# Second score matmul over 128 rows instead of 64, exponentials in place, and fewer buffers, in a hybrid decoder block

## The chip, the cores and the metric

The kernel runs on one core of one Trainium2 chip. The metric is the device time of one execution in microseconds (us); lower is better. The kernel before is a Tile program: the code below is traced once, a scheduler puts each engine's instructions into one fixed order, and at run time every engine works through its own list in that order and waits on semaphores for the others. The engines are TensorE (PE, whose weight loads the profile lists apart as PEld), VectorE (DVE), ScalarE (ACT) and GpSimd (POOL); SyncE (SP) issues all the DMAs.

## The reference, cut to what matters

One decoder block over 1024 tokens of width 1024: an RMSNorm and one large projection, then two attention branches whose outputs are gated, merged and projected, then a SwiGLU feed-forward. The change touches the two attention branches alone:

```python
# branch A, sparse: 8 heads of 64; every query row attends to its own 256 keys
sc = jnp.einsum('bqhd,bqkhd->bhqk', qb, kg) * att_scale
p = softmax(where(valid, sc, -inf));  out = p @ vg
# branch B, differential: 4 heads of two maps, 64 dims each
sc = jnp.einsum('bqhmd,bshmd->bhmqs', qb, k) * scale
a = softmax(where(causal, sc, -inf))
a = a[:, :, 0] - lam * a[:, :, 1];  out = a @ v
...
merged = gates[:, :, 0] * (o_a @ w_branch_dsa) + gates[:, :, 1] * (o_b @ w_branch_diff)
```

Everything is float32. The kernel keeps precision by splitting a number into a high part, which the TensorE format float32r holds, and a low part, the rest; a product is then hi x hi + lo x hi + hi x lo.

## The kernel before, in words

The kernel runs in stages that follow each other on TensorE: transposes and index projection; the large projections (L427, L505) with the sparse branch's key selection beside them on VectorE; from 529 us the attention; from 843 us the merge (L632) and the output projection (L882); and the feed-forward (L933, L914) to the end.

Attention consists of 32 units of the differential branch (4 heads, 8 blocks of 128 queries each, the longest rows first) and then 64 units of the sparse branch (8 heads, 8 blocks each). A loop (L803) emits for step i the parts of several units, each part with a lag in steps: the scores of a unit at lag 0, the combination of its maps or its division at lag 1, its transposes and its product with v later. In the differential branch a unit has two maps, m = 0 and m = 1.

`scores` (L586) fills a PSUM tile `big` (two of them) with the scores of one map for one block, of up to two halves of up to 512 columns. For each half there are two matmuls that accumulate in the same place:

- L593 contracts 128 rows. Its weights are the query tile `qs`, in which the 64 rows of this map's own half (rows m*64 to m*64+63) hold the high part and the other 64 the low part (`load_maps`, L530). Its moving operand `khs` holds the high part of the keys twice, in rows 0 to 63 and in 64 to 127. So it gives q_hi x k_hi + q_lo x k_hi.
- L594 contracts the 64 rows `own` alone, where `qs` holds the high part of the queries and `kls` the low part of the keys: q_hi x k_lo. One `kls` tile serves two maps, each in its own 64 rows.

Then VectorE adds the mask, takes the row's extreme and writes the masked scores to an SBUF tile `ms` (L651 in the differential branch, L703 in the sparse one; `ms` has 3 buffers). ScalarE reads `ms` and writes the exponentials (L656, L707) to another tile: `pm0`, 3 buffers, or for map 1 one of the 4 `wide` buffers. The transposed tiles and one square (L684) also live in `wide`. The differential branch combines the two maps on VectorE (L671 to L674), TensorE transposes (L603) and multiplies with v (L610), and ScalarE copies both out (L604, L682). The sparse branch scales (L713, L715), transposes (L729), splits into two parts (L730, shown as L101 on ACT and L102 on DVE) and multiplies (L742).

At the end of each differential head its outputs, one `gt` tile of 4 KB a partition (pool `gst`, 2 buffers), are squared, normed (L685 to L690), transposed (L617) and split. During the sparse branch the differential branch's projection (L770) runs in 16 half chunks; it needs the 4 tiles of w_bdiff in both parts. `Weights.get` (L121) makes these: a DMA into a raw tile, a copy to the high part on ACT (L101), a subtraction to the low part on POOL (L102). The pool `w2` has one raw buffer of its own for that. The weights w_bdsa of the other projection are loaded likewise near the end of attention, two through the raw buffer and two through `gt` tiles.

SP's queue is one list: the loads of the next head's queries and keys, of its v, and of the weights stand in one order, and a load whose buffer is still in use holds up all that stand behind it.

Of the kernel before, what the change touches and what calls it, by code (L numbers as in the profile page):

```python
# [18 lines left out]
P = 128  # L19
# [7 lines left out]
# block whose scores are kept negated and in reverse, so that the few left out are taken away instead  # L27
# [23 lines left out]
def block_kernel(ctx, tc, x, pos, g_mix, w_qk, w_v, q_scale, w_idx, w_gate, ikg, ikb, lams, sub_g, gate_b,  # L51
# [19 lines left out]
    # constants  # L71
# [32 lines left out]
    # scratch in DRAM  # L104
    # rows (dim, map): maps 0-7 are queries, 8-15 keys
# [3 lines left out]
    # sparse branch: per head the two parts of v, high part first in even heads, last in odd ones  # L109
# [21 lines left out]
    # rows of tokens -> RMSNorm * gain, then both parts of the transpose  # L131
# [9 lines left out]
    def to_T(h, hi, lo, wide=False):  # L141
        # hi, lo: [P, KC, P] views
# [34 lines left out]
    def rope(eng, pool, xv, tabs, half, **kw):  # L177
        # xv: [P, ..., d] view; tabs: c0, c1, s0, s1 broadcast to the rotated halves
# [176 lines left out]
    # rotary tables: [c | c] and [-s | s] per position  # L355
# [43 lines left out]
    # lambda (on every partition), negated  # L399
# [130 lines left out]
    def load_maps(br, h):  # L530
        kl_ = stk.tile([P, S], F32R, name="kls", bufs=2)
        for m in range(2):
            q = stk.tile([P, S], F32R, name="qs")
            kh_ = stk.tile([P, S], F32R, name="khs")
            for j in range(2):
                rows = slice(j * 64, j * 64 + 64)
                nc.sync.dma_start(q[rows].bitcast(F32), (qk_hi if j == m else qk_lo)[br][:, 2 * h + m, :])
                nc.sync.dma_start(kh_[rows].bitcast(F32), qk_hi[br][:, 8 + 2 * h + m, :])
            own = slice(m * 64, m * 64 + 64)
            nc.sync.dma_start(kl_[own].bitcast(F32), qk_lo[br][:, 8 + 2 * h + m, :])  # L540
            maps[br, 2 * h + m] = q, kh_, kl_, own
# [9 lines left out]
    def load_head(br, h):  # L551
        # diff: head h has two maps; sparse: a pair of heads
# [21 lines left out]
    at = ExitStack()  # L574
    W2 = Weights(at.enter_context(tc.tile_pool(name="w2", bufs=1)), 1, 4)
# [4 lines left out]
    # the other branch's projection runs in half chunks, one every EVERY units of the sparse branch; until it  # L580
    # is through, the sparse outputs (head pairs below PARKED) wait in DRAM
# [4 lines left out]
    def scores(mp, t):  # L586
        q, kh_, kl_, own = mp
# [3 lines left out]
        for u in range(nh):  # L591
            cols = slice(u * w, u * w + n)
            T.matmul(sp_[:, u, :n], lhsT=q[:, t * P:(t + 1) * P], rhs=kh_[:, cols], start=True, stop=False)  # L593
            T.matmul(sp_[:, u, :n], lhsT=q[own, t * P:(t + 1) * P], rhs=kl_[own, cols], start=False, stop=True)  # L594
# [52 lines left out]
    def diff_Q(u, m):  # L647
        sv, nh = scores(maps[0, 2 * u.h + m], u.t)
        ms = ap_.tile([P, S], F32, name="ms", bufs=3)
# [389 lines left out]
```

## Time and profile before

| | us |
|---|---|
| median of 3 runs | 1743.11 (1740.65 to 1744.91) |
| span of the profiled execution | 1738.8 |
| attention in it, first score matmul to the merge | 529 to 843 |
| differential branch | 529 to 653 |
| sparse branch | 653 to 843 |

The profiled execution's own time stands in no list beside the span; the median of the runs is 4.3 us above the span, and that difference is taken for what lies around it. TensorE is busy for 98% of the span. Busy is not the same as streaming, though: a matmul counts as busy from its recorded start to its modelled end, so in a stretch that reads 100% the distance from one matmul's start to the next one's start tells how long it really held the engine.

### The profile page before, as it was taken

How to read it: one execution, taken by the hardware profiler on the slowest of the kernel's cores; microseconds unless marked ns; L12 is line 12 of the kernel's file. 1: busy time of each engine (PE TensorE's matmuls, PEld its weight loads, DVE VectorE, ACT ScalarE, POOL GpSimd, SP SyncE). 2: the span in 40 equal slices, each digit the busy share in tenths (PEclk: the TensorE clock that was granted, in tenths of full speed). 3: DMA queues.
4: the chain of work that ended last, by engine and by line, in shares of the span. 5: the costliest groups of instructions: out<-in, count | busy, mean ns of one | idle time of the engine just before them, and what ended most of it. 6: DMA issues, size and time to landing. Idle time of an engine off the chain costs nothing.

```text
span 1738.8 us, 22187 instructions
## 1 busy us (share of the span) xinstructions
PE 1699.2 (98%) x8552; PEld 1397.9 (80%) x8552; DVE 1103.3 (63%) x1901; ACT 571.9 (33%) x1035; POOL 422.1 (24%) x313
## 2 busy tenths in 40 slices
PE   7799999999999999999999999999999999999998
PEld 7688789988886677777789978888888888888886
DVE  6589999989997887777661534443443444444435
ACT  5444531221115777667520421111111111111113
POOL 2532521432201132113312222212212212211211
PEclk9999999999998999999999999999999999999999
DMA  4243342475312546544471121111111111111102
GB/s 163 88 146 110 122 139 92 134 198 153 106 52 62 124 112 159 154 137 146 149 257 49 43 79 49 61 37 49 61 37 45 56 47 37 51 59 37 37 12 97
DMA packets 69641, 162.74 MB, mean 94 GB/s; under 512 B 8096, under 2 KB 25632, under 8 KB 69536
## 3 DMA queue, kind: packets, MB, share of 16 engines
q1 hardware_dynamic: 69536, 161.33, 29.8%
q8 instruction: 67, 1.10, 0.3%
q14 instruction: 38, 0.31, 0.1%
HBM read 118.31 MB, written 42.99 MB: 93 GB/s over the span
## 4 chain that ended last, share of the span: by engine, by line
PE 86%; DVE 8%; issue 2%; DMA 1%; POOL 1%; ACT 1%; SPq 0%; DVEq 0%; POOLq 0%; ACTq 0%
PE big L933 28%; PE big L427 10%; PE tr L914 7%; PE mm L914 7%; PE mm L505 5%; PE mm L882 5%; PE mm L427 5%; PE big L594 4%; PE big L593 3%; PE mm L770 3%; PE mm L742 2%; PE mm L610 2%; PE tr L729 2%; DVE score L300 1%; DVE score L277 1%
## 5 line engine op out<-in xcount | busy, mean ns | idle before, releaser
L102 POOL TENSOR_TENSOR wlo<-raw,whi 128x1024 fp32r<-128x1024 f32 (+1 forms) x121 | 293.0, 2425 | 948.3 <-ACT whi L101 937.8
L101 ACT ACTIVATE whi<-raw 128x1024 fp32r<-128x1024 f32 (+1 forms) x124 | 129.7, 1048 | 523.8 <-issue 231.1
L918 DVE TENSOR_TENSOR x<-tr,x 128x512 f32<-128x512 f32 x168 | 115.7, 689 | 178.5 <-PE tr L914 178.0
L933 PE MATMUL big<-actC,whi 128*128 128x512 f32 x704 | 221.8, 395 | 0.0
L933 PE MATMUL big<-actA,whi 128*128 128x512 f32 x704 | 217.8, 390 | 0.0
L943 DVE TENSOR_TENSOR si<-big,si 128x512 f32<-128x512 f32 x44 | 30.4, 692 | 232.7 <-PE big L933 232.7
L299 DVE MAX8 m<-score 128x8 f32<-128x640 f32 (+5 forms) x176 | 162.6, 924 | 5.4 <-POOL score L283 0.4
L300 DVE MATCH_REPLACE8 score<-m,score 128x640 f32<-128x640 f32 (+5 forms) x176 | 159.5, 906 | 0.0
L933 PEld LDWEIGHTS big<-actC,whi 128*128 128x128 f32 x704 | 132.0, 188 | 32.0 <-ACT si L938 0.3
L933 PEld LDWEIGHTS big<-actA,whi 128*128 128x128 f32 x704 | 132.0, 188 | 28.9 <-ACT si L938 0.5
L933 PE MATMUL big<-actC,wlo 128*128 128x512 f32 x352 | 139.1, 395 | 0.0
L933 PE MATMUL big<-actA,wlo 128*128 128x512 f32 x352 | 137.1, 390 | 0.0
L918 DVE TENSOR_TENSOR x<-mm,x 128x512 f32<-128x512 f32 x168 | 115.6, 688 | 0.7
L914 PE MATMUL tr<-whi,actB 128*128 128x512 f32 x352 | 110.6, 394 | 0.0
L914 PE MATMUL mm<-whi,actB 128*128 128x512 f32 x352 | 110.4, 395 | 0.0
L427 PE MATMUL mm<-hT_hi,whi 128*128 128x512 f32 x256 | 102.4, 400 | 2.4 <-DVE st_lo L489 2.4
L427 PE MATMUL mm<-hT_lo,whi 128*128 128x512 f32 x256 | 100.8, 394 | 0.0
L427 PE MATMUL mm<-hT_hi,wlo 128*128 128x512 f32 x256 | 100.7, 393 | 0.0
L427 PE MATMUL big<-hT_hi,whi 128*128 128x512 f32 x256 | 99.6, 389 | 0.0
L427 PE MATMUL big<-hT_lo,whi 128*128 128x512 f32 x256 | 99.6, 389 | 0.0
L427 PE MATMUL big<-hT_hi,wlo 128*128 128x512 f32 x256 | 99.6, 389 | 0.0
L101 ACT ACTIVATE actB<-si 128x512 fp32r<-128x512 f32 x44 | 27.9, 634 | 196.8 <-DVE si L943 196.8
(237 smaller groups left out, 3541.6 us busy)
## 6 DMA issues: line engine op xcount, KB each, us to landing
raw<-in_w_ffi_dram SPq DMA_DIRECT2D x44, 512.0 KB, 3.4
raw<-in_w_ffo_dram SPq DMA_DIRECT2D x22, 512.0 KB, 3.4
raw<-in_w_qk_dram SPq DMA_DIRECT2D x16, 512.0 KB, 3.3
qkh<-st_hi SPq DMA_DIRECT2D x32, 256.0 KB, 2.0
qkl<-st_lo SPq DMA_DIRECT2D x32, 256.0 KB, 2.2
raw<-in_w_gate_dram SPq DMA_DIRECT2D x16, 512.0 KB, 4.3
khs<-qkh SPq DMA_DIRECT2D x32, 256.0 KB, 5.5
gdr<-gt SPq DMA_DIRECT2D x16, 512.0 KB, 3.6
```

The lines of the kernel that those rows point to most:

```text
L101: A.activation(hi, src, AF.Copy)
L102: lo_eng.tensor_sub(lo, src, hi.bitcast(F32))
L299: tc.keep_in_program_order(V.max(m8, work[t]))
L300: V.match_replace(work[t], m8, work[t], GONE)
L427: T.matmul(dst, lhsT=w[b][:, k * P:(k + 1) * P], rhs=hT[a][:, k, u * 512:(u + 1) * 512], start=n == 0, stop=n == 23)
L505: T.matmul(pt[:, tt, :], lhsT=hT[a][:, k, t * P:(t + 1) * P], rhs=wt[w0 + k // 4][b][:, (k % 4) * 256:(k % 4) * 256 + 256], start=n == 0, ...
L593: T.matmul(sp_[:, u, :n], lhsT=q[:, t * P:(t + 1) * P], rhs=kh_[:, cols], start=True, stop=False)
L594: T.matmul(sp_[:, u, :n], lhsT=q[own, t * P:(t + 1) * P], rhs=kl_[own, cols], start=False, stop=True)
L882: T.matmul(pt[:, :256], lhsT=act[a][:, k, i % 4 * P:i % 4 * P + P], rhs=wot[2 * q + k // 4][b][:, (k % 4) * 256:(k % 4) * 256 + 256], star ...
L914: T.matmul(pt, lhsT=a_[a][:, i * P:(i + 1) * P], rhs=w[b][:, u * 512:(u + 1) * 512], start=n == 0, stop=n == 3 * len(items) - 1)
L918: V.tensor_add(x2[i][:, sl], pt, x2[i][:, sl])
L933: T.matmul(gu[:, j, :], lhsT=w[b][:, k * P:(k + 1) * P], rhs=h2[u][a][:, k, :], start=n == 0, stop=n == 23)
```

## The change

- `load_maps` loads the low part of the keys twice, into both halves of a `kls` tile of its own for each map (4 buffers of 4 KB instead of 2), and the second score matmul contracts all 128 rows of `qs` and `kls`. It adds q_lo x k_lo to the scores, which the kernel before left out. Columns and number of the matmuls stay.
- The tiles `ms` and `pm0` (3 buffers each) become one tile `pm` with 5: VectorE writes the masked scores to it and ScalarE writes the exponentials over them. For map 1 of the differential branch both go to the `wide` buffer, which is so taken at the mask and no longer at the exponential.
- The raw buffer of the pool `w2` is gone. All eight weight tiles of the two branch projections are loaded into `gt` tiles, of which there are two.

Per partition that is 8 KB more, and 4 KB and 4 KB less. In the changed file the lines from L531 on carry numbers lower by one to three (L593 for L594, L650 for L651, L767 for L770).

```diff
     def load_maps(br, h):
-        kl_ = stk.tile([P, S], F32R, name="kls", bufs=2)
         for m in range(2):
             q = stk.tile([P, S], F32R, name="qs")
             kh_ = stk.tile([P, S], F32R, name="khs")
+            kl_ = stk.tile([P, S], F32R, name="kls")
             for j in range(2):
                 rows = slice(j * 64, j * 64 + 64)
                 nc.sync.dma_start(q[rows].bitcast(F32), (qk_hi if j == m else qk_lo)[br][:, 2 * h + m, :])
                 nc.sync.dma_start(kh_[rows].bitcast(F32), qk_hi[br][:, 8 + 2 * h + m, :])
-            own = slice(m * 64, m * 64 + 64)
-            nc.sync.dma_start(kl_[own].bitcast(F32), qk_lo[br][:, 8 + 2 * h + m, :])
-            maps[br, 2 * h + m] = q, kh_, kl_, own
+                nc.sync.dma_start(kl_[rows].bitcast(F32), qk_lo[br][:, 8 + 2 * h + m, :])
+            maps[br, 2 * h + m] = q, kh_, kl_
...
-    W2 = Weights(at.enter_context(tc.tile_pool(name="w2", bufs=1)), 1, 4)
+    W2 = Weights(at.enter_context(tc.tile_pool(name="w2", bufs=1)), 0, 4)
...
             T.matmul(sp_[:, u, :n], lhsT=q[:, t * P:(t + 1) * P], rhs=kh_[:, cols], start=True, stop=False)
-            T.matmul(sp_[:, u, :n], lhsT=q[own, t * P:(t + 1) * P], rhs=kl_[own, cols], start=False, stop=True)
+            T.matmul(sp_[:, u, :n], lhsT=q[:, t * P:(t + 1) * P], rhs=kl_[:, cols], start=False, stop=True)
...
     def diff_Q(u, m):
         sv, nh = scores(maps[0, 2 * u.h + m], u.t)
-        ms = ap_.tile([P, S], F32, name="ms", bufs=3)
+        pm = ap_.tile([P, 2, S], F32, name="wide", bufs=4)[:, 0, :] if m else ap_.tile([P, S], F32, name="pm", bufs=5)
...
-        pm = ap_.tile([P, 2, S], F32, name="wide", bufs=4)[:, 0, :] if m else ap_.tile([P, S], F32, name="pm0", bufs=3)
         sm = small.tile([P, 1], F32, name="sm")
-        A.activation(pm[:, :u.ext], ms[:, :u.ext], AF.Exp, bias=mx, scale=-1.0, accum_out=sm)
+        A.activation(pm[:, :u.ext], pm[:, :u.ext], AF.Exp, bias=mx, scale=-1.0, accum_out=sm)
...
-                u.wb.extend(W2.get(w_bdiff[k]) for k in range(4))
+                u.wb.extend(W2.get(w_bdiff[k], raw=gst.tile([P, S], F32, name="gt")) for k in range(4))
...
     def dsa_A(u):
-        ms = ap_.tile([P, S], F32, name="ms", bufs=3)
-        msv = ms[:, :u.ext].rearrange("p (u w) -> p u w", u=nh)
+        u.pm = ap_.tile([P, S], F32, name="pm", bufs=5)
+        msv = u.pm[:, :u.ext].rearrange("p (u w) -> p u w", u=nh)
...
-        u.pm = ap_.tile([P, S], F32, name="pm0", bufs=3)
-        A.activation(u.pm[:, :u.ext], ms[:, :u.ext], AF.Exp, bias=mx, scale=-1.0, accum_out=u.sm)
+        A.activation(u.pm[:, :u.ext], u.pm[:, :u.ext], AF.Exp, bias=mx, scale=-1.0, accum_out=u.sm)
...
-            wa.extend(W2.get(w_bdsa[k], raw=None if k % 2 else gst.tile([P, S], F32, name="gt")) for k in range(4))
+            wa.extend(W2.get(w_bdsa[k], raw=gst.tile([P, S], F32, name="gt")) for k in range(4))
```

The order of most engines stays nearly as it was. Two places change. The first is SP's queue: the last of the four loads of w_bdiff stood before the loads of the sparse heads (`qkh_77` there is the sparse branch's keys), and the other three earlier. Before:

```order
L538 DMA khs<-qkh_76 64x1024
L540 DMA kls<-qkl_78 64x1024
L547 DMA vt<-vsdr 128x8x128
L125 DMA raw<-in_w_bdiff_dram 128x1024
L538 DMA khs<-qkh_77 64x1024
L537 DMA qs<-qkh_77 64x1024
L537 DMA qs<-qkl_79 64x1024
```

Now, in the queue of the changed kernel, all four stand among the loads of the second sparse pair, the first of them behind that pair's first load:

```order
L546 DMA vt<-vsdr 128x8x128
L538 DMA khs<-qkh_77 64x1024
L125 DMA gt<-in_w_bdiff_dram 128x1024
L537 DMA qs<-qkh_77 64x1024
L539 DMA kls<-qkl_79 64x1024
L537 DMA qs<-qkl_79 64x1024
L125 DMA gt<-in_w_bdiff_dram 128x1024
L538 DMA khs<-qkh_77 64x1024
L539 DMA kls<-qkl_79 64x1024
L537 DMA qs<-qkl_79 64x1024
L125 DMA gt<-in_w_bdiff_dram 128x1024
```

So the four loads moved from the course of the differential branch to its end. The second place is POOL's list at the same point. Before, the last two low parts of w_bdiff (`wlo<-raw`) stood between the norms of the first three heads (L685, L690):

```order
L690 TENSOR_TENSOR gt<-gt,rs_5166 128x1024
L102 TENSOR_TENSOR wlo<-raw,whi 128x1024
L685 TENSOR_TENSOR wide<-gt 128x1024
L98 TENSOR_TENSOR rs_5535<-rs_v,nhalf 128x8
L690 TENSOR_TENSOR gt<-gt,rs_5535 128x1024
L102 TENSOR_TENSOR wlo<-raw,whi 128x1024
L685 TENSOR_TENSOR wide<-gt 128x1024
L98 TENSOR_TENSOR rs_5904<-rs_v,nhalf 128x8
L690 TENSOR_TENSOR gt<-gt,rs_5904 128x1024
```

Now all four follow the norm of the third head (the first row here); the first two stand ahead of the fourth head's norm (L683, L688), the last two behind it:

```order
L688 TENSOR_TENSOR gt<-gt,rs_5863 128x1024
L102 TENSOR_TENSOR wlo<-gt,whi 128x1024
L720 MEMSET wide 128x128 x2
L102 TENSOR_TENSOR wlo<-gt,whi 128x1024
L683 TENSOR_TENSOR wide<-gt 128x1024
L720 MEMSET wide 128x128 x2
L98 TENSOR_TENSOR rs_6210<-rs_v,nhalf 128x8
L688 TENSOR_TENSOR gt<-gt,rs_6210 128x1024
L720 MEMSET wide 128x128 x2
L102 TENSOR_TENSOR wlo<-gt,whi 128x1024
L102 TENSOR_TENSOR so_6278<-aux,so_6277 64x256
```

The low parts moved behind the norms; on TensorE the first half chunk of the projection that reads them keeps its place, around the transposes of the fourth head.

## Rows read from the trace of the kernel before

**Rows 1.** Page, busy time, share of the span and instructions of each engine.

```profile
PE 1699.2 (98%) x8552; PEld 1397.9 (80%) x8552; DVE 1103.3 (63%) x1901; ACT 571.9 (33%) x1035; POOL 422.1 (24%) x313
```

**Rows 2.** Busy us of each engine in eight stretches of attention, then TensorE's granted clock.

```profile
529.00:561.00 32.00, 32.00 (x126) 20.63 (x126) 21.99 (x62) 21.88 (x47) 3.52 (x2) 0.79 0.17 54
561.00:577.00 16.00, 16.00 (x72) 9.74 (x71) 10.85 (x27) 10.77 (x25) 1.74 (x1) 1.00 0.74 157
577.00:592.00 15.00, 15.00 (x99) 12.03 (x99) 14.49 (x40) 11.28 (x31) 5.54 (x4) 1.00 0.36 104
592.00:607.00 15.00, 15.00 (x67) 9.11 (x65) 10.50 (x27) 10.92 (x26) 2.27 (x1) 1.00 0.70 143
607.00:622.00 15.00, 15.00 (x96) 11.81 (x96) 14.48 (x40) 11.34 (x30) 5.43 (x3) 1.00 0.32 96
622.00:637.00 15.00, 15.00 (x70) 9.24 (x68) 10.47 (x30) 10.89 (x26) 2.36 (x1) 1.00 0.71 150
637.00:653.00 16.00, 16.00 (x104) 12.56 (x103) 15.47 (x42) 11.43 (x31) 5.42 (x3) 1.00 0.33 97
653.00:843.00 190.00, 188.48 (x1005) 139.65 (x1004) 145.61 (x365) 135.61 (x323) 48.97 (x97) 0.99 0.51 142
```

**Rows 3.** Timeline of PE: start us, length us, what, idle time before it.

```profile
559.66 0.36 PE L593 MATMUL big<-khs,qs 128*128 128x256 f32 x1
559.96 0.38 PE L594 MATMUL big<-kls,qs 64*128 64x256 f32 x1
560.27 1.38 PE L610 MATMUL mm<-vt,wide 128*128 128x128 f32 x10
561.41 0.48 PE L593 MATMUL big<-khs,qs 128*128 128x512 f32 x1
561.82 0.49 PE L594 MATMUL big<-kls,qs 64*128 64x512 f32 x1
562.24 0.49 PE L593 MATMUL big<-khs,qs 128*128 128x512 f32 x1
```

**Rows 4.** Timeline of PEld, the weight loads of the last two matmuls above.

```profile
561.82 0.18 PEld L594 LDWEIGHTS big<-kls,qs 64*128 64x128 f32 x1 [0.24 <-issue]
562.24 0.19 PEld L593 LDWEIGHTS big<-khs,qs 128*128 128x128 f32 x1 [0.24 <-issue]
```

**Rows 5.** Timeline of PE where 128-row matmuls follow one another in the sparse branch.

```profile
692.25 2.14 PE L742 MATMUL mm<-wide,vt 128*128 128x256 f32 x16
694.23 0.40 PE L770 MATMUL mm<-oT_hi,whi 128*128 128x512 f32 x1
694.46 0.40 PE L770 MATMUL mm<-oT_lo,whi 128*128 128x512 f32 x1
```

**Rows 6.** Groups by line, PEld, 653:843: count, busy us, mean ns, idle before.

```profile
L770 PEld LDWEIGHTS mm<-oT_lo,whi 128*128 128x128 f32 x64 | 12.1, 188 | 1.7
```

**Rows 7.** Line L594's matmuls: count and ns min/median/max, first and last start.

```profile
L594 PE MATMUL big<-kls,qs x192: 378/442/686, 529.0 to 836.7; 64*128 64x512 f32 x48, 64*128 64x384 f32 x48, 64*128 64x448 f32 x32, 64*128 64x320 f32 x32
```

**Rows 8.** Groups by line, DVE, 529:653; last is the idle time before and its releaser.

```profile
L651 DVE CUSTOM_DVE_ANT_0 ms<-big,causw 128x1024 f32<-128x1024 f32 (+7 forms) x64 | 47.8, 748 | 21.8 <-PE big L594 21.7
```

**Rows 9.** Timeline of PE: the third head's transposes and the projection's first matmul.

```profile
649.97 1.09 PE L617 MATMUL tr<-ident,gt 128*128 128x128 f32 x8
...
674.67 0.40 PE L770 MATMUL mm<-oT_hi,whi 128*128 128x512 f32 x1
```

**Rows 10.** Timeline of SP's queue: the first load of the second sparse pair.

```profile
649.76 0.45 SPq L538 DMA_DIRECT2D khs<-qkh  x1
```

**Rows 11.** The four loads of w_bdiff: issue ns min/median/max, first and last, landing.

```profile
L125 SPq DMA_DIRECT2D raw<-in_w_bdiff_dram x4: 333/429/527, 528.9 to 607.2; - x4
...
DMA to landing us min/median/max: 3.4/4.2/4.9
```

**Rows 12.** Timeline of ACT: the high part of one w_bdiff tile.

```profile
542.20 1.04 ACT L101 ACTIVATE whi<-raw 128x1024 fp32r<-128x1024 f32 x1
```

**Rows 13.** Timeline of POOL: the low part of one w_bdiff tile.

```profile
560.32 2.42 POOL L102 TENSOR_TENSOR wlo<-raw,whi 128x1024 fp32r<-128x1024 f32 x1 [14.15 <-ACT whi L101]
```

More of the change, by code (lines that the diff above doesn't have):

```diff
@@ L586, in scores @@
     def scores(mp, t):
-        q, kh_, kl_, own = mp
+        q, kh_, kl_ = mp
         nh, w = halves(t)
@@ L648, in diff_Q @@
         sv, nh = scores(maps[0, 2 * u.h + m], u.t)
-        ms = ap_.tile([P, S], F32, name="ms", bufs=3)
+        pm = ap_.tile([P, 2, S], F32, name="wide", bufs=4)[:, 0, :] if m else ap_.tile([P, S], F32, name="pm", bufs=5)
         mx = small.tile([P, 1], F32, name="mx")
-        V.tensor_tensor_reduce(ms[:, :u.ext].rearrange("p (u w) -> p u w", u=nh), sv,
+        V.tensor_tensor_reduce(pm[:, :u.ext].rearrange("p (u w) -> p u w", u=nh), sv,
                                causw[:, S - u.ext:].rearrange("p (u w) -> p u w", u=nh), 1.0,
                                -FILL, OP.add, OP.min, accum_out=mx)
-        pm = ap_.tile([P, 2, S], F32, name="wide", bufs=4)[:, 0, :] if m else ap_.tile([P, S], F32, name="pm0", bufs=3)
         sm = small.tile([P, 1], F32, name="sm")
-        A.activation(pm[:, :u.ext], ms[:, :u.ext], AF.Exp, bias=mx, scale=-1.0, accum_out=sm)
+        A.activation(pm[:, :u.ext], pm[:, :u.ext], AF.Exp, bias=mx, scale=-1.0, accum_out=sm)
         u.pm.append(pm)
```

## The prediction, made before the changed kernel was run

> **What bounds the kernel now.** I read the page's busy times first: TensorE is busy for 98% of the span, VectorE for 63% [rows 1]. So time can only be won on TensorE, or lost by a wait that TensorE does not have now. The change touches attention alone, so next come the busy times by stretch [rows 2]. TensorE reads 100% in nearly all of it, VectorE between 66% and 97%, ScalarE about 70%. A busy TensorE need not stream, so I then read the starts in its timeline. Where score matmuls alternate, from a 128-row L593 to a 64-row L594 and back, 512 columns are 0.41 to 0.42 us from start to start; for 256 columns it is 0.30 and 0.31 [rows 3]. Where 128-row matmuls follow one another, 512 columns take 0.23 us, and sixteen of 256 columns take 1.98 us, 0.124 each [rows 5]. So a score matmul holds the engine some 0.185 us longer than its columns need, whatever its width. The weight loads say why: each of the score loads starts at the same time as its matmul, after the load unit sat idle for 0.24 us, and takes 0.18 to 0.19 us [rows 4]. The loads of L770 take as long (188 ns) and have next to no idle time before them [rows 6]: they run under the matmul before. So the load is exposed where the number of rows switches between 128 and 64, and hidden where it stays.
>
> **The change part by part.**
>
> *Second matmul over 128 rows.* There are 192 of L594 [rows 7], as many L593, and half of each lies in either branch (8 maps or heads with 12 halves each). Columns stay, the switch goes: 384 x 0.185 = 71 us less of TensorE's time, 35.5 in each branch. The first matmul after a score gains a little too; I leave that for the range. What is late next decides how much of the 71 us reaches the end, so I take the branches apart.
>
> Differential branch, 529 to 653, 124 us. TensorE would need 124 - 35.5 = 88.5, VectorE's sum over the seven stretches is 98.3 and ScalarE's 88.5 [rows 2]. In three of them (577 to 592, 607 to 622, 637 to 653; 46 us, the short query blocks) VectorE already is at 97%: nothing to win there. In the other four, 78 us, VectorE is busy for 53.8 and ScalarE for 54.5. At the 97% that VectorE now reaches in its full stretches that would be 56 us; since two engines that feed each other would both have to be full, I take 92%, 59 us. Gain 19, between 10 (both at 80%) and 26 (VectorE without a gap). VectorE's present wait for L594, 21.7 us over 64 reductions [rows 8], is the cover that this uses up.
>
> In the first stretch TensorE's granted clock averages 0.79 [rows 2], so it ran at the lower of its two levels (1.2 GHz) for some 13 of the 32 us (32 x 0.21 / 0.5). If the clock stays up there now, that is part of these 19 us and not more, since VectorE paces the stretch.
>
> Sparse branch, 653 to 843, 190 us. TensorE needs 190 - 35.5 - 1.5 (its present idle) = 153, VectorE 145.6, ScalarE 135.6 [rows 2]. TensorE stays the bound, with VectorE close behind. At 95% of TensorE that is 161: gain 29, between 15 and 37 (no gap at all).
>
> *Keys loaded twice.* 16 more loads of 256 KB on SP, 0.45 us or a little more of its queue each [rows 10], 7 us in all, spread over the loads of 8 heads and pairs. Nothing: the loop asks for them a whole head ahead, and that head (some 30 us, 124 / 4) is the cover; a head whose loads came late would cost the lateness, at most 1 us each.
>
> *Exponentials over the scores.* Same number, shape and engine of instructions. Map 1 now takes its `wide` buffer at the reduction, so VectorE instead of ScalarE waits for that buffer, that is for a product with v four units back, with the next reductions, and through them TensorE's `big`, queued behind. No row shows that wait. The nearest is VectorE's wait for scores, 0.34 us per reduction [rows 8]; 32 of these would be 11 us, the other end is a gain of the same kind, since map 0 has five buffers instead of three. I take 0, as TensorE will be ahead of VectorE in this branch.
>
> *w_bdiff through the `gt` tiles.* This is the part that costs. Today the four loads go out between 529 and 607 us [rows 11], and all is ready 50 us before the first L770 at 674.67 [rows 9]. Now the first load stands in SP's queue behind the first load of the second sparse pair, which went out at 649.76 [rows 10], and needs the `gt` tile that the third head's transposes free at 649.97 + 1.09 [rows 9]. The other `gt` tile holds the fourth head's output until its own transposes, which stand between the projection's eighth and ninth matmul. So all four go through one tile, one after another: issue 0.5, landing 4.2 [rows 11], high part 1.04 [rows 12], low part 2.42 [rows 13], and about 0.8 of hand-overs by my estimate: 9 us each. The third high part is there 18 + 5.7 = 24 us after the start, the fourth low part after 36. The projection's first matmul comes 24 us after the start today; with less in between on TensorE and VectorE I expect 18. Its seventh matmul needs the third high part, its twelfth the fourth low part some 5 us later: TensorE would wait 6 at the first and 5 to 7 more by the last, 13 at most. ScalarE has the four copies in its list with exponentials behind them; the wait is the same chain, not a second one. Part of it falls where TensorE would have waited for VectorE anyway, so I take 8 of 0 to 13. w_bdsa goes the same way at the end, through two tiles that are both free, when nine of the 64 units are left (9 x 190 / 64 = 27 us) to cover two steps of 9 us: nothing.
>
> *Sum.* -19 - 29 + 8 = -40 us on the profiled execution's span of 1738.8, 1699; with the 4 us by which the runs' median lies over that span, 1703.
>
> **A rule against it.** Rows 4 and 6 show a weight load that waits for the matmul before it and one that does not. The Trainium skill (TensorE: Matmul & The Clock Gate, "What overlaps and what doesn't") says that a load overlaps a running matmul only when its row group differs. By that rule a 128-row load would be exposed behind a 128-row matmul too, and the new pairs would take 0.42 us as the old ones do; L770's loads [rows 5, 6] speak against it.
>
> **The rivals.**
>
> *The distance stays (slower).* If the pairs stay at 0.42 us, because the exposed load hangs on something else in them than the number of rows (weights that are read twice, accumulation into one bank), nothing is won on TensorE, and the chain of w_bdiff costs its 8 to 13 us: 1743 + 10 = 1753. It decides for slower as soon as less than 8 us of the 71 come through. For it: no row shows two 128-row score matmuls in a row. Against: L770 accumulates into one bank as well and L742 changes weights for each matmul, both at full pace [rows 5]. In the sentence above the page's rule gives this same time.
>
> *TensorE's gain comes through whole.* VectorE and ScalarE run without gaps, the chain hides behind VectorE's backlog: -26 - 37 = -63, 1680. For it: VectorE does reach 97% in three stretches. Against: in these, TensorE had no slack of its own to lose.
>
> *New waits eat most of it.* Attention becomes a ring of three nearly full engines with two `big` tiles: gains of 10 and 15, the chain at its full 13: -12, 1731. For it: VectorE's and ScalarE's sums are so close to TensorE's new one. Against: TensorE runs at 99% today with VectorE at 77%.
>
> **How the numbers follow.** Forecast 1703 (within about 15): 0.62. Whole gain, 1680: 0.14. New waits, 1731: 0.15. Distance stays, 1753: 0.09. The range leaves out the last case and the far ends of the next two: 1684 to 1731. About 0.3%, 5 us, is what a measurement can tell from no change. Under 1738 lie the first two cases and most of the third: faster 0.87; same 0.05; slower 0.08.
>
> **What would show it.** In the new trace, 512-column scores start 0.23 us after one another where TensorE does not wait, and the loads of the second matmul have no 0.24 us of idle before them; if not, the first step is wrong. In the differential branch VectorE is at 90% and more and TensorE waits for `big` on VectorE, in about 105 us; the sparse branch takes about 169 us with the chain. TensorE waits at the projection's seventh to twelfth matmul for the high and low parts of w_bdiff; if these waits are missing, the chain was priced too high. The prediction is wrong if ScalarE's blocked list or the `wide` buffers stop VectorE by more than 10 us in either branch, or if the clock falls to its lower level in stretches where TensorE now waits.

## The result, and the profile after

The changed kernel takes 1701.5 us, the median of four runs (1700.1 to 1703.2); the kernel before, in the same comparison, 1741.9 (1739.5 to 1744.9). The ratio is 0.9762, with a 95% interval from 0.9738 to 0.9786: 40 us faster. The forecast was 1703, in a range from 1684 to 1731. The profiled execution spans 1701.5 us, against 1738.8.

The page's busy times and its chain of waits answer to [rows 1]. TensorE's busy share falls from 98% to 96%. In the chain TensorE has 76% of the span and VectorE 13%; the page of before has 86% and 8%.

```profile
PE 1639.8 (96%) x8552; PEld 1392.5 (82%) x8552; DVE 1097.4 (64%) x1901; ACT 568.7 (33%) x1035; POOL 421.8 (25%) x313
...
PE 76%; DVE 13%; DMA 3%; issue 3%; ACT 2%; POOL 2%; SPq 0%; DVEq 0%; POOLq 0%; ACTq 0%
```

The first question is the distance of the score matmuls. The timeline of PE at the start of attention shows the changed kernel's first scores (L592 and L593 are the old L593 and L594) behind the last projection matmuls (L427):

```profile
528.50 0.39 PE L427 MATMUL big<-hT_lo,whi 128*128 128x512 f32 x1
528.73 0.40 PE L427 MATMUL big<-hT_hi,wlo 128*128 128x512 f32 x1
528.96 0.39 PE L592 MATMUL big<-khs,qs 128*128 128x512 f32 x1
529.19 0.39 PE L593 MATMUL big<-kls,qs 128*128 128x512 f32 x1
529.42 0.39 PE L592 MATMUL big<-khs,qs 128*128 128x512 f32 x1
529.64 0.39 PE L593 MATMUL big<-kls,qs 128*128 128x512 f32 x1
```

All are 0.22 or 0.23 us from start to start, where [rows 3] had 0.41 and 0.42. The weight loads of these lines in the sparse branch (the last columns are count, busy us and mean ns of one, then the idle time ahead of them, all together) still take 0.19 us each. The 96 loads of L593 have 0.9 us of idle ahead of them in sum; in [rows 4] a single one had 0.24:

```profile
L593 PEld LDWEIGHTS big<-kls,qs 128*128 128x128 f32 x96 | 18.3, 191 | 0.9
L592 PEld LDWEIGHTS big<-khs,qs 128*128 128x128 f32 x95 | 18.0, 190 | 6.3 <-DVE mx L701 4.8 <-PE mm L739 0.3
```

So the load is no shorter: it lies under the matmul before it.

The stretches of attention answer to [rows 2] (busy us of PE, PEld, DVE, ACT and POOL, then the granted clock, the DMA share and GB/s):

```profile
529.00:561.00 32.00, 29.74 (x190) 25.03 (x189) 28.56 (x84) 27.46 (x65) 0.00 (x0) 1.00 0.38 87
561.00:575.00 14.00, 11.87 (x92) 10.71 (x91) 14.00 (x42) 11.10 (x31) 5.44 (x3) 1.00 0.53 107
575.00:600.00 25.00, 22.58 (x164) 20.47 (x163) 24.43 (x68) 20.72 (x54) 5.44 (x3) 1.00 0.69 148
600.00:638.00 38.00, 34.13 (x241) 29.99 (x239) 36.35 (x99) 31.65 (x81) 8.11 (x6) 1.00 0.72 163
638.00:660.00 22.00, 16.40 (x91) 12.47 (x90) 14.58 (x34) 15.96 (x36) 15.50 (x14) 0.88 0.67 171
660.00:680.00 20.00, 20.00 (x125) 17.98 (x124) 16.20 (x41) 15.12 (x38) 4.40 (x12) 0.96 0.64 182
680.00:780.00 100.00, 96.93 (x614) 84.29 (x613) 85.47 (x216) 77.77 (x184) 23.12 (x55) 1.00 0.67 176
780.00:805.00 25.00, 23.02 (x135) 19.32 (x134) 20.64 (x55) 22.18 (x53) 13.11 (x18) 0.86 0.46 165
```

In the differential branch, which now ends at 628 us, VectorE is busy for 89% to 100%, and TensorE has gaps of 7% to 15%. In the sparse branch TensorE is nearly full, but for 638 to 660, where it is busy for 16.4 of 22 us, and 780 to 805; its granted clock falls to 0.88 and 0.86 in these two stretches. In the first of them the projection's first half chunk waits for its weights. SP's issues of the four loads of w_bdiff, and the half chunk's matmuls from the seventh on:

```profile
625.88 0.35 SPq L125 DMA_DIRECT2D gt<-in_w_bdiff_dram  x1
633.29 0.35 SPq L125 DMA_DIRECT2D gt<-in_w_bdiff_dram  x1
641.08 0.33 SPq L125 DMA_DIRECT2D gt<-in_w_bdiff_dram  x1
651.03 0.33 SPq L125 DMA_DIRECT2D gt<-in_w_bdiff_dram  x1
```

```profile
648.61 0.39 PE L767 MATMUL mm<-oT_hi,whi 128*128 128x512 f32 x1
648.83 0.39 PE L767 MATMUL mm<-oT_lo,whi 128*128 128x512 f32 x1
651.05 0.50 PE L767 MATMUL mm<-oT_hi,wlo 128*128 128x512 f32 x1 [0.47 <-POOL wlo L102]
656.08 0.79 PE L767 MATMUL mm<-oT_hi,whi 128*128 128x512 f32 x1 [2.82 <-ACT whi L101]
656.67 0.63 PE L767 MATMUL mm<-oT_lo,whi 128*128 128x512 f32 x1
658.53 0.80 PE L767 MATMUL mm<-oT_hi,wlo 128*128 128x512 f32 x1 [0.17 <-POOL wlo L102]
```

The ninth waits for the third low part, the tenth for the fourth high part, the twelfth for the fourth low part. From the first (647.23) to the twelfth it is 11.3 us; before it was 5.9.

For the comparisons below attention is cut at two events that all versions have: from VectorE's first score reduction of the differential branch to its first of the sparse branch ("differential"), and from there to the first matmul of the output projection, L879 in the changed kernel and L882 before ("sparse").

| us | before | after | difference |
|---|---|---|---|
| differential | 124.3 | 98.3 | -26.0 |
| sparse, to the output projection | 235.2 | 222.3 | -12.9 |
| all else in the span | 1379.3 | 1380.9 | +1.6 |
| span | 1738.8 | 1701.5 | -37.3 |

The time came from where it was expected. It is divided otherwise: the differential branch gave 26 and not 19, the sparse branch with the chain of weights 13 and not 21.

Among the runs of the next section, one of e3 (3221.5 us) and one of e6 (5765.9 us) lie far from the others of their kernel and are left out of medians and ratios.

### The profile page after: what moved, and what is told of

Same layout as the page of the kernel before. It is cut to its first block, busy times and chain, and to the rows that moved or that the text cites. A ratio compares the mean times of both kernels' runs of the same rounds, so it can differ in the third digit from the quotient of the medians.

```text
span 1701.5 us, 22157 instructions
## 1 busy us (share of the span) xinstructions
PE 1639.8 (96%) x8552; PEld 1392.5 (82%) x8552; DVE 1097.4 (64%) x1901; ACT 568.7 (33%) x1035; POOL 421.8 (25%) x313
## 4 chain that ended last, share of the span: by engine, by line
PE 76%; DVE 13%; DMA 3%; issue 3%; ACT 2%; POOL 2%; SPq 0%; DVEq 0%; POOLq 0%; ACTq 0%
PE big L930 28%; PE big L427 10%; PE tr L911 7%; PE mm L911 7%; PE mm L505 5%; PE mm L879 5%; PE mm L427 5%; DVE score L300 1%; DVE score L277 1%; PE mm L767 1%; PE mm L739 1%; DVE m L299 1%; DMA gt<-gdr 1%; POOL wlo L102 1%; PE tr L726 1%
## 5 line engine op out<-in xcount | busy, mean ns | idle before, releaser
L102 POOL TENSOR_TENSOR wlo<-raw,whi 128x1024 fp32r<-128x1024 f32 (+1 forms) x115 | 278.0, 2422 | 871.5 <-ACT whi L101 861.1
L101 ACT ACTIVATE whi<-raw 128x1024 fp32r<-128x1024 f32 (+1 forms) x118 | 123.4, 1048 | 508.3 <-issue 232.4
L911 PE MATMUL mm<-whi,actB 128*128 128x512 f32 x352 | 110.4, 395 | 0.0
L427 PE MATMUL mm<-hT_hi,whi 128*128 128x512 f32 x256 | 102.4, 400 | 2.4 <-DVE st_lo L489 2.4
L427 PE MATMUL mm<-hT_lo,whi 128*128 128x512 f32 x256 | 100.9, 394 | 0.0
L427 PE MATMUL mm<-hT_hi,wlo 128*128 128x512 f32 x256 | 100.6, 393 | 0.0
L427 PE MATMUL big<-hT_hi,whi 128*128 128x512 f32 x256 | 99.6, 389 | 0.0
L427 PE MATMUL big<-hT_lo,whi 128*128 128x512 f32 x256 | 99.6, 389 | 0.0
L427 PE MATMUL big<-hT_hi,wlo 128*128 128x512 f32 x256 | 99.6, 389 | 0.0
```

The costliest lines, as they stand in the source:

```text
L101: A.activation(hi, src, AF.Copy)
L102: lo_eng.tensor_sub(lo, src, hi.bitcast(F32))
L427: T.matmul(dst, lhsT=w[b][:, k * P:(k + 1) * P], rhs=hT[a][:, k, u * 512:(u + 1) * 512], start=n == 0, stop=n == 23)
L911: T.matmul(pt, lhsT=a_[a][:, i * P:(i + 1) * P], rhs=w[b][:, u * 512:(u + 1) * 512], start=n == 0, stop=n == 3 * len(items) - 1)
```

## The experiments

| kernel | median us | ratio to before, 95% | differential | sparse | first half chunk |
|---|---|---|---|---|---|
| before | 1741.9 | 1 | 124.3 | 235.2 | 5.9 |
| after | 1701.5 | 0.9738 to 0.9786 | 98.3 | 222.3 | 11.3 |
| e1_rows64 | 1755.6 | 1.0048 to 1.0091 | 126.6 | 246.4 | 11.2 |
| e2_both64 | 1731.2 | 0.9900 to 0.9948 | 110.4 | 238.5 | 10.8 |
| e3_one_mm | 1695.3 | 0.9694 to 0.9742 | 96.0 | 213.8 | 10.8 |
| e4_spread | 1701.8 | 0.9733 to 0.9785 | 104.7 | 212.2 | 5.2 |
| e5_b_raw | 1750.5 | 1.0028 to 1.0059 | 125.7 | 244.7 | 10.9 |
| e6_b_inplace | 1746.6 | 1.0016 to 1.0042 | 125.1 | 238.5 | 5.2 |
| e7_raw_pm4 | 1693.8 | 0.9686 to 0.9729 | 101.1 | 213.0 | 5.2 |
| e8_shift2 | 1706.6 | 0.9769 to 0.9812 | 98.3 | 225.7 | 5.7 |
| e9_pm4 | 1701.4 | 0.9751 to 0.9780 | 98.3 | 222.1 | 10.7 |
| e10_after | 1700.6 | 0.9740 to 0.9769 | 98.3 | 221.7 | 11.8 |
| e11_raw_pm4 | 1695.0 | 0.9706 to 0.9738 | 102.2 | 211.9 | 5.2 |
| e12_rows_only | 1709.6 | 0.9773 to 0.9838 | 112.0 | 216.8 | 5.4 |

The last column is the time from the first to the twelfth matmul of the projection's first half chunk. Kernels e1 to e4, e5 to e8, e9 to e11, and e12 ran on one chip each, beside the kernel before, which took 1744.4, 1742.7, 1742.9 and 1740.2 us there. So a distance between two kernels of different groups is good to some 2 or 3 us.

**One part undone: 64 rows again.** The changed kernel, with the second matmul on the map's own 64 rows as before; all else stays.

```diff
-            T.matmul(sp_[:, u, :n], lhsT=q[:, t * P:(t + 1) * P], rhs=kl_[:, cols], start=False, stop=True)
+            T.matmul(sp_[:, u, :n], lhsT=q[own, t * P:(t + 1) * P], rhs=kl_[own, cols], start=False, stop=True)
```

> The changed kernel with one thing undone: the second score matmul contracts the 64 rows of its own half again (the keys' low part is still loaded twice, buffers as changed; q_lo x k_lo is left out as in the kernel before). Theory: a weight load is exposed where the number of rows switches. Then score matmuls of 512 columns are 0.42 us apart again, the differential branch takes 120 to 124 us instead of 98, and the time is that of the kernel before, 1742, plus 0 to 8 for the chain of w_bdiff loads. Rival: the gain comes from the buffers (five for the masked scores, exponentials in place); then the time stays under 1715.

It took 1755.6 us. The distance is back, in the timeline of PE at the start of this kernel's attention:

```profile
533.36 0.50 PE L593 MATMUL big<-kls,qs 64*128 64x512 f32 x1
533.79 0.49 PE L592 MATMUL big<-khs,qs 128*128 128x512 f32 x1
534.21 0.49 PE L593 MATMUL big<-kls,qs 64*128 64x512 f32 x1
534.63 0.50 PE L592 MATMUL big<-khs,qs 128*128 128x512 f32 x1
```

So the number of rows alone is worth 1755.6 - 1701.5 = 54 us (53 by the ratios), and the other parts of the change cost 11 to 12 together (ratio 1.0069).

**The switch, or the 64 rows?** Both matmuls on the same 64 rows: no switch between them, though one from and to the transposes and products around them. It leaves out q_lo x k_hi and q_lo x k_lo.

```diff
-            T.matmul(sp_[:, u, :n], lhsT=q[:, t * P:(t + 1) * P], rhs=kh_[:, cols], start=True, stop=False)
-            T.matmul(sp_[:, u, :n], lhsT=q[:, t * P:(t + 1) * P], rhs=kl_[:, cols], start=False, stop=True)
+            T.matmul(sp_[:, u, :n], lhsT=q[own, t * P:(t + 1) * P], rhs=kh_[own, cols], start=True, stop=False)
+            T.matmul(sp_[:, u, :n], lhsT=q[own, t * P:(t + 1) * P], rhs=kl_[own, cols], start=False, stop=True)
```

> The changed kernel with both score matmuls on the same 64 rows (it leaves out q_lo x k_hi and q_lo x k_lo). Theory (the switch costs): inside a row of scores nothing switches, 512 columns are 0.23 us apart, the load is exposed only on entering and leaving a row of scores, some 100 times each, 0.1 to 0.2 us: the time is 1702 to 1720. Rival (64 rows themselves expose the load): 0.42 us apart throughout and 1740 to 1750.

The same place of this kernel, the last matmul of 128 rows and then four of 64:

```profile
528.47 0.39 PE L427 MATMUL big<-hT_hi,wlo 128*128 128x512 f32 x1
528.79 0.50 PE L592 MATMUL big<-khs,qs 64*128 64x512 f32 x1
529.12 0.39 PE L593 MATMUL big<-kls,qs 64*128 64x512 f32 x1
529.36 0.39 PE L592 MATMUL big<-khs,qs 64*128 64x512 f32 x1
529.59 0.39 PE L593 MATMUL big<-kls,qs 64*128 64x512 f32 x1
```

Matmuls of 64 rows run at the full pace too, 0.23 and 0.24 apart; only the first pays (0.32 to it, and 0.33 behind it). So it is the switch that costs, not the 64 rows. Behind the last score matmul of a group, where TensorE goes back to 128 rows, the median distance of 512 columns is 0.32 us, against 0.23 in the changed kernel. The time, 1731.2, missed its expectation by 11 us: it lies 30 us above the changed kernel's, where 18 were allowed for the switches. TensorE's order is that of the changed kernel but for two matmuls, so the two can be compared matmul by matmul. Where neither waits or runs at the lower clock, the starts of this one lie 35 us further apart in sum, 17.6 in the differential branch and 17.4 in the sparse one, all of it beside a change of rows. TensorE's waits between the first score and the last fall from 20.6 to 6.7 us and take up 14 of these. So the switches were under-priced: some 21 us of them are left, for at most 18 expected. Four stretches of 6.8 us at the lower clock (at 535, 648, 668 and 719 us; the changed kernel has two in attention) lie on the same side; what they cost is not settled.

**What VectorE leaves.** The changed kernel without the second score matmul at all; it leaves out the low part of the keys.

> The changed kernel without the second score matmul (the keys' low part is left out). Theory: after the change VectorE paces the differential branch, so it takes 98 us as in the changed kernel (96 to 99), though TensorE has 17 us less to do there; in the sparse branch TensorE is nearly the bound, so of 17 us less some 5 to 12 come through. Time 1688 to 1697. Rival: TensorE still paces both branches; then both get 10 to 17 us shorter and the time is 1668 to 1680.

Half of the score matmuls are gone, and the differential branch is only 2.3 us shorter (96.0 for 98.3). The sparse part is 8.5 us shorter (213.8 for 222.3), the whole 6 by the medians. In the differential branch TensorE is now busy for 82% and VectorE for 97% (columns as in the stretches above):

```profile
532.00:628.00 96.00, 78.45 (x525) 66.05 (x525) 92.92 (x263) 81.36 (x207) 16.31 (x9) 0.95 0.39 92
```

So the branch isn't TensorE's any more. What would still be to win there by faster scores is some 2 us.

**The chain of weights, by an earlier start.** The changed kernel with its w_bdiff loads spread over the ends of the first three differential heads.

```diff
-            if u.h == 2:
-                u.wb.extend(W2.get(w_bdiff[k], raw=gst.tile([P, S], F32, name="gt")) for k in range(4))
+            ks = ((0, 1), (2,), (3,), ())[u.h]
+            u.wb.extend(W2.get(w_bdiff[k], raw=gst.tile([P, S], F32, name="gt")) for k in ks)
```

> The changed kernel with the four w_bdiff loads spread: two are asked for after the first differential head, one after the second, one after the third, each in the gt tile that is free then. Theory: TensorE's waits at the projection's seventh to twelfth matmul come from the four loads going through one tile one after another at 7 to 10 us each, and with the lower clock after them cost 6 to 10 us; the time is 1692 to 1696. Rival: these waits fall where TensorE would wait for VectorE anyway; then the time stays within 2 us of 1701.5, while the waits are gone.

The waits in the half chunk are gone (5.2 us for 11.3), the sparse part is 10 us shorter, the differential branch 6.4 longer, and the time is the same: the rival's outcome. One price of it is visible, though not how much of the 6.4 us it makes: the low parts now run on POOL beside VectorE, in the branch where VectorE is the bound. The timeline of POOL, then that of VectorE around it:

```profile
583.02 2.40 POOL L102 TENSOR_TENSOR wlo<-gt,whi 128x1024 fp32r<-128x1024 f32 x1 [7.72 <-ACT whi L101]
```

```profile
583.23 2.20 DVE L670 SCALAR_TENSOR_TENSOR cf<-sm,nlam,cf 128x1 f32<-128x1 f32 x1
585.47 0.35 DVE L672 SCALAR_TENSOR_TENSOR pm<-wide,cf,pm 128x128 f32<-128x128 f32 x1
...
587.00 0.22 DVE L670 SCALAR_TENSOR_TENSOR cf<-sm,nlam,cf 128x1 f32<-128x1 f32 x1
```

An operation on one column took 2.20 us and ended with POOL's subtraction, at 585.43; the next one, alone, took 0.22. The Trainium skill (SBUF — State Buffer, "SBUF: two separate sides") says that a VectorE operation with two SBUF inputs and a GpSimd operation that reads SBUF exclude each other for a whole instruction; these rows, in which both read SBUF tiles, agree.

**The chain alone.** The kernel before, with only the raw buffer taken away, as in the change.

```diff
-    W2 = Weights(at.enter_context(tc.tile_pool(name="w2", bufs=1)), 1, 4)
+    W2 = Weights(at.enter_context(tc.tile_pool(name="w2", bufs=1)), 0, 4)
...
-                u.wb.extend(W2.get(w_bdiff[k]) for k in range(4))
+                u.wb.extend(W2.get(w_bdiff[k], raw=gst.tile([P, S], F32, name="gt")) for k in range(4))
...
-            wa.extend(W2.get(w_bdsa[k], raw=None if k % 2 else gst.tile([P, S], F32, name="gt")) for k in range(4))
+            wa.extend(W2.get(w_bdsa[k], raw=gst.tile([P, S], F32, name="gt")) for k in range(4))
```

> The kernel before with one part of the change alone: all eight weight tiles go through the gt tiles and the raw buffer is gone; 64-row second matmul and separate ms and pm0 tiles stay. Theory: the chain of w_bdiff is what made the changed kernel with its 64-row matmul undone (1755.6) slower than the kernel before, so this one is 6 to 11 us slower than the kernel before, with TensorE waiting at the projection's seventh to twelfth matmul. Rival: exponentials in place cost it; then this one is within 3 us of the kernel before.

It is slower by 0.43% of 1742.7, 7.5 us. The half chunk takes 10.9 us, and what its line L770 waited for (us, times) is the chain again; waits of its weight loads and of its matmuls both count here, and TensorE's own make 3.5 us of the 8:

```profile
  ACT whi L101: 5.2, 2
  POOL wlo L102: 2.8, 4
```

**The exponentials in place alone.** The kernel before, with one tile `pm` of five buffers in place of `ms` and `pm0` with three each, and map 1 in `wide` from the mask on.

> The kernel before with another part alone: exponentials over the masked scores, five pm tiles instead of three ms and three pm0; raw buffer and 64-row second matmul stay. Theory: no effect, within 3 us of the kernel before, VectorE's wait for products with v under 3 us. Rival: taking the wide buffer at the reduction holds VectorE up; then 4 to 11 us slower.

It is slower by 0.29%, 5 us (3 to 7): so it is not nothing, and the size is the rival's. The rival's wait is there too, VectorE's for the product with v that holds a `wide` buffer (total us, times, longest); the kernel before has none:

```profile
DVE wide L651 <- PE mm L610: 2.3, 3, 0.8
```

But it is under the 3 us that the theory allowed, and it does not explain the loss: the differential branch, the only one where it can occur, is 0.8 us longer, the sparse part 3.3. What costs those is not shown. With the 7.5 us of e5 it makes 12.5, about the 11 to 12 that e1 left for all parts but the rows.

**The space given to the raw buffer.** The changed kernel, with the raw buffer kept and four `pm` tiles instead of five, which takes the same space.

```diff
-    W2 = Weights(at.enter_context(tc.tile_pool(name="w2", bufs=1)), 0, 4)
+    W2 = Weights(at.enter_context(tc.tile_pool(name="w2", bufs=1)), 1, 4)
...
-        pm = ap_.tile([P, 2, S], F32, name="wide", bufs=4)[:, 0, :] if m else ap_.tile([P, S], F32, name="pm", bufs=5)
+        pm = ap_.tile([P, 2, S], F32, name="wide", bufs=4)[:, 0, :] if m else ap_.tile([P, S], F32, name="pm", bufs=4)
...
-                u.wb.extend(W2.get(w_bdiff[k], raw=gst.tile([P, S], F32, name="gt")) for k in range(4))
+                u.wb.extend(W2.get(w_bdiff[k]) for k in range(4))
```

> The changed kernel with the raw buffer kept and one pm tile fewer (4 instead of 5), which takes the same space. Theory: the chain is gone from the sparse branch (its second head takes 24 us instead of 31), but the four low parts on POOL now fall into the differential branch, where VectorE is full, and lengthen it by 3 to 6 us, as in the run with the loads spread; time 1698 to 1702, the same as the changed kernel. Rival: the space is better spent on the raw buffer; 1690 to 1696. Or four pm tiles are too few: over 1706.

I expected no difference, and was wrong: 1693.8 us, faster than both kernels, as the rival had it. Its stretches (the differential branch and the sparse one), and under them the same of the changed kernel:

```profile
531.00:632.00 101.00, 89.09 (x621) 78.84 (x620) 96.91 (x263) 84.91 (x211) 26.30 (x13) 1.00 0.63 146
633.00:796.00 163.00, 155.19 (x983) 134.06 (x982) 142.15 (x358) 131.87 (x316) 47.34 (x95) 0.99 0.63 174
```

```profile
529.00:627.00 98.00, 88.77 (x620) 78.68 (x618) 93.34 (x263) 81.97 (x206) 16.31 (x9) 1.00 0.57 122
628.00:797.00 169.00, 156.89 (x970) 133.54 (x969) 140.26 (x354) 132.49 (x311) 55.13 (x97) 0.97 0.67 184
```

POOL's 10 us for the four low parts are back in the differential branch, where they cost VectorE some 3 us. In exchange TensorE no longer waits for weights at the start of the sparse branch: that part is 9 us shorter, and its clock is 0.99 instead of 0.97.

**Half chunks two steps later.** The changed kernel, with the projection's half chunks in the third unit of each three instead of the first, so that the weights have time to come. In this version the last half chunk reads the fourth sparse pair's outputs where those of the fourth differential head belong; the amount of work is the same.

```diff
-            u.chunk = n // EVERY if n % EVERY == 0 and n // EVERY < 2 * KC else None
+            u.chunk = n // EVERY if n % EVERY == 2 and n // EVERY < 2 * KC else None
```

> The changed kernel with the projection's half chunks two units later (units 2, 5, ... 47 instead of 0, 3, ... 45); the loads of w_bdiff stay after the differential branch. Theory: the chain then has some 5 us more before its readers come, TensorE's waits in the first half chunk fall from 8 to under 4 us and nothing is put into the differential branch: 1695 to 1699. Rival: as with the loads spread, what is saved there is lost elsewhere: within 2 us of the changed kernel.

The half chunk no longer waits for w_bdiff (5.7 us), but nothing is won: 1706.6 us, by the ratios 0.3% above the changed kernel, with intervals that overlap. What TensorE waits for from 630 to 800 us (total us, times, longest) shows where it went:

```profile
PE mm L739 <- ACT wide L101: 4.2, 2, 4.0
PE tr L726 <- DVE pm L712: 2.4, 4, 1.3
PE mm L767 <- POOL oT_lo L102: 2.0, 1, 2.0
```

The sparse branch's own product with v (L739) waits for ScalarE once for 4.0 us, where the changed kernel's longest wait of that kind was 0.4 us. That ScalarE's list was held up there by a copy of w_bdiff is my reading; no run takes that copy alone away.

**Which of the two parts of e7?** The changed kernel with four `pm` tiles and no raw buffer, the changed kernel itself, and e7's version again, on one chip.

> The changed kernel with four tiles for the exponentials instead of five; all weights still go through the one gt tile. Theory (the raw buffer, not the number of these tiles, made the version with both faster): within 3 us of the changed kernel, 1699 to 1705; the first half chunk's first twelve matmuls still take 10 to 12 us, and the differential branch 98 to 100. Rival (the fifth tile itself does harm, by letting VectorE's reductions run ahead of the combinations): 1692 to 1697, with the first half chunk as slow as before.

> The changed kernel again, beside the others on one chip: 1699 to 1705 by either theory; it gives the distance of the two versions on the same chip.

> The changed kernel with the raw buffer kept and four tiles for the exponentials, again, beside the changed kernel on one chip. If its advantage is real: 1691 to 1697, 5 to 10 us under the changed kernel. If it came from the chip of the first call: within 3 us of the changed kernel.

They took 1701.4, 1700.6 and 1695.0 us. The fifth `pm` tile is worth nothing either way; the raw buffer, with four such tiles in both (e9 and e11), is worth 6.4 us, again at 5.2 us for the first half chunk in place of 10.7.

**Rows of 128 without the exponentials in place.** As e7's version in space and weights, but with `ms` and `pm0` apart, in two buffers each (three do not fit beside the larger `kls`).

> The kernel before with the 128-row matmul and the keys' low part loaded twice, its raw buffer kept, and the exponentials still in tiles of their own; the space comes from two buffers each of ms and pm0 instead of three. It takes as much space as the version with the raw buffer and four tiles in place, which took 1694 and 1695. Theory (writing the exponentials over the scores is a price, as the 4.8 us in the 64-row kernel): 1687 to 1692. Rival (it costs nothing once VectorE paces the differential branch, and the four tiles serve better in place than two and two): 1694 to 1702.

It took 1709.6 us, 15 more than e7's version (14 to 17 by the ratios): slower even than the rival's 1694 to 1702, and the theory of a price in place falls for this space. The differential branch is 10 us longer. What VectorE waited for in attention has this first row, of a kind that e7's version doesn't have among its ten longest; ScalarE's wait under it says why (total us, times, longest):

```profile
DVE rc L668 <- ACT pm L655: 11.2, 11, 3.5
```

```profile
ACT pm L655 <- PE tr L602: 18.7, 22, 2.9
```

The exponential of map 0 waits for a `pm0` buffer, which is held until the transposes of an earlier unit have read it, and VectorE, the bound, waits for that exponential. Writing in place lets four tiles do what two and two can't. Whether it would still cost 4 or 5 us against three and three, as in the 64-row kernel, can't be tried in this space.

## Why the prediction was right

**The exposed load: right.** It was priced at 0.185 us for each of 384 score matmuls; the distance of 512 columns fell from 0.42 to 0.23, and e1 brings it back. Summed over the median distances by width and place, TensorE's work falls by 35 us in the differential branch (35.5 expected) and by 32 in the sparse one. The near hit is in part luck: the score matmuls alone give some 31 and 29 of it, and the rest comes from the transposes and products beside them, which the prediction had left for the range. What the score matmuls miss stands at the first of a group: behind transposes, and in the differential branch behind the products, 512 columns go from 0.41 to 0.32 us and not to 0.23; behind the sparse branch's products they go to 0.23, but were at 0.32 before. No run takes apart why 0.09 us stay behind the former, whose operands are float32 and whose matmuls have 128 columns. e2 adds that the switch is the cause. The first rival, by which the distance stays, is out, and with it the rule of the Trainium skill named in the prediction (TensorE: Matmul & The Clock Gate, "What overlaps and what doesn't"): 128-row loads lie under 128-row matmuls here.

**The differential branch: the mechanism right, the size too small.** VectorE became the bound, as said. The branch gave 26 us, which was the outer bound, but not in the way of that bound. VectorE is not without gaps: it is busy for 93.3 of 98 us, 95%. What moved is its sum, from the 98.3 us of [rows 2] (of which the lowest share is 68%, not the prediction's 66%) to 93.3; the prediction held that sum fixed and took 92% of it in the four long stretches. That the two met at 26 is luck. The reductions answer to [rows 8]. Their two forms, to 627 us, wait 2.8 us together, where 64 waited 21.8:

```profile
L650 DVE CUSTOM_DVE_ANT_0 pm<-big,causw 128x1024 f32<-128x1024 f32 (+7 forms) x32 | 23.9, 747 | 2.5 <-PE big L593 2.4
...
L650 DVE CUSTOM_DVE_ANT_0 wide<-big,causw 128x1024 f32<-128x1024 f32 (+7 forms) x31 | 23.6, 762 | 0.3 <-PE big L593 0.2
```

So 3 to 4 of the 7 us go with POOL's low parts of w_bdiff, which moved out of the branch: the versions that keep them there take 101.1 (e7) and 102.2 us (e11), and VectorE's sum in e7 is 96.9. The rest is that VectorE reaches 95% and not 92%. The clock did what was expected for the first stretch: 1.00 from 529 to 561, where [rows 2] have 0.79.

**The sparse branch: the mis-sized term.** It was put at -29 without the chain. The version without the chain of waits (e7) shows -22 (213.0 for 235.2), and the step from e1 to the changed kernel, both with the chain, -24. TensorE's row of before from the branch's first reduction to the first matmul of the merge (at 838 us; 843 in [rows 2] lies some matmuls into it) stands against e7's second row above:

```profile
654.00:838.00 184.00, 182.60 (x966) 135.14 (x967) 141.55 (x355) 129.99 (x309) 47.80 (x94) 0.99 0.52 145
```

Its busy time fell by 27 us, from 182.6 to 155.2, and its idle time rose from 1.4 to 7.8. The idle time was foreseen (95% of TensorE); the fall of the busy time was taken at 35.5. By the starts it is 32, as above; the rest is most likely waiting that reads busy, since a matmul's recorded end lies past the next one's start. So of the 7 us about half is work, since not every score matmul lost a whole load, and half is waiting beyond the 8 us that the 95% allowed for.

**The chain: right.** +8 was taken, of 0 to 13. In e5 it costs 7.5 us; between the changed kernel and e7 it is 9 in the sparse part. Of these 9, some 6 are in the half chunk itself (11.3 for 5.2 us). Its steps were 7.4, 7.8 and 10 us, for 9 expected. The projection began 19 us after the branch did, for 18 expected. The waits stand at the ninth, tenth and twelfth matmul, not at the seventh: the third high part was ready. The chain's removal gives back only 6 us net, since POOL's work then falls on VectorE's branch.

**Exponentials in place: taken as 0.** In the 64-row kernel it costs 5 us, within the ends of -11 to 11. In the changed kernel it can't be separated; there it is what makes the space do. VectorE's wait for a `wide` buffer, which the prediction feared, is not among the waits of the changed kernel; it waits 1.2 us for `pm` tiles in the sparse branch.

**Keys loaded twice, w_bdsa: 0, right** as far as the trace shows: TensorE has no wait for a load of `khs` or `kls` in attention, and none for w_bdsa at the merge.

**The sum.** -26 - 22 + 9 = -39 in the two parts, beside -19 - 29 + 8 = -40: the 7 us too little in one branch met the 7 too much in the other, so the forecast came closer than its terms, by luck. It happened once more: the span came to 1701.5 us, 2.5 above the sum's 1699, but the 4 us added for what lies around the span are 1.7 in each run (the profiled run took 1703.2). Most of the 4.3 before was then the distance between one run and the median. The second rival (1680) fails at the sparse branch, the third (1731) at VectorE, which needs no slack to run full.

**The clock: the prediction's own sign of being wrong came.** It named a fall to the lower level where TensorE now waits. At 655 and 795 us TensorE runs at that level for 6.8 us each, behind the waits for w_bdiff and among waits for VectorE and ScalarE at the end of the branch. It does not make the attention slower in sum, since the differential branch gave back 13.7 us at the lower level in its first stretch: in attention there were some 17 us of it before and 13.6 now. In e10 the second fall is missing, and the sparse part is 0.6 us shorter than in the changed kernel's first profile (221.7 for 222.3), so this one costs little; the price of the first stays open.

## What to carry to other kernels

Read the distance from one matmul's start to the next, not the busy share: a stream that changes between 64 and 128 contracted rows pays an exposed weight load at each change, which a busy TensorE hides from the page. When it is gone, cost each stage by the engine that is next, at the share that it reaches elsewhere in the kernel (here 95% to 97%), and ask first whether its own sum stays: here work that another engine did beside it had moved away. A buffer taken away to make room can cost more than its tile: see in which order its loads, copies and readers follow one another, and try what each other tile of the same size is worth (here the fifth of a kind was worth nothing).

## What the runs showed of the hardware

- A weight load of 128 columns is recorded with 0.18 to 0.19 us at 64 and at 128 rows. It is hidden at 64 behind 64 (0.23 to 0.24 us for 512 columns, e2) as at 128 behind 128, and exposed at a change in either direction (0.41 to 0.43 us where every matmul changes, e1; 0.32 and 0.33 on the two sides of a single change, e2). Behind float32 matmuls of 128 columns, 0.09 us stay without a change of rows (0.32 us in the changed kernel).
- A VectorE operation on a single column lasted 2.20 us beside a POOL subtraction of 2.40, and 0.22 without it (e4). Four such subtractions more beside a full VectorE go with 3 to 4 us more in its branch (e7, e11).
- The granted clock fell to its lower level where TensorE had waited, at 655 us in the changed kernel, and stayed up at 529 to 561 (not in e11, which has 3.4 us at the lower level there), where the kernel before, busy by the page for the whole stretch but with exposed loads, was granted 0.79.
